# Sample rows of a hybrid decoder step: retention for four heads at once, search products read in PSUM, bias by one-hot products

## The chip, the cores and the metric

The program runs on one core of a Trainium2 chip. The metric is the device time of one execution in microseconds (us). Matmuls and transposes run on TensorE (PE in the profile; PEld is its weight load), elementwise work on VectorE (DVE), ScalarE (ACT) and GpSimd (POOL). SyncE (SP) issues most DMA transfers; POOL issues the gathers, whose row numbers lie in a tile. Every engine works through its own list in order. Matmul results lie in PSUM, of which the kernel uses eight banks; all other tiles lie in SBUF.

## What is computed

One layer of a decoder for two groups of rows that share the weights: a prompt of 1024 positions and 8 sample rows, one for each of 8 sequences with 2048 past positions. First FFN, one projection, sparse attention beside retention, output projection, second FFN, with a layer norm after each. The parts that the change touches belong to the sample rows:

```python
# retention, 4 heads of 128x128 state; for one new position of each sequence:
att = einsum('bihd,bjhd->bhij', qc, kc) * intra
o = einsum('bhij,bjhv->bihv', att, vc) + einsum('bihd,bhdv->bihv', qc, s) * cross_decay
s_new = chunk_decay * s + einsum('bjhd,jh,bjhv->bhdv', kc, kv_decay, vc)
# sparse attention: the 256 best of 2049 keys by the indexer's score, then
logits = einsum('bqhd,bqkhd->bhqk', q, k_sel) * DH_A ** -0.5
bias = rel_bias[t5_bucket(qpos - idx)]          # rel_bias: 32 buckets x 8 heads
p = softmax(where(valid, logits + bias, -inf)); out = einsum('bhqk,bqkhd->bqhd', p, v_sel)
```

A bucket is the number of 31 rising thresholds that the distance reaches.

## The kernel before, in words

All 1032 rows are held transposed, features in the partitions, in three chunks of 344 rows. A product in full precision is made of three fast ones of high and low parts (L169 to L171, L403 to L405). Each weight arrives by SP's transfers (L228), ACT makes its high part (L273) and DVE its low part (L274); up to four raw weights are fetched ahead.

The work is written as generators that a small planner interleaves (`Sched`). The dense products are the main line: each adds its estimated PE time to a clock (`tick`, `g.s.t`), and a generator that gave a delay with `yield` goes on once that time has passed. So the `yield` numbers set where in the program each step of a side job stands. A later pass may move instructions of an engine past each other by its own estimates.

Three side jobs matter. `sret` (L1190) updates the retention state of the sample rows, one sequence after the other, beside the projections of q, k and v: PE spreads a row of v over the partitions (L1069, into a PSUM bank), then for each of four heads ACT multiplies it by that head's key column (L1223, into one small tile `kv`) and DVE adds it to the decayed state (L1224). After a delay the state is stored (L1226), multiplied by the query (L1228), and the state of the sequence after the next is loaded (L1231) into the same half of `sra`.

`s2_select` (L1608) finds the 256 keys of each sequence. Its last part (L1691 on) searches, for each sequence and each half of 128 slots, the position of the selected key: a product into a PSUM bank (L1696), an ACT copy (L1697), four DVE steps (L1698 to L1701). Then the distances become buckets (L1708 to L1710), and 16 gathers on POOL's queue fetch a row of 8 floats of `rel_bias` for each of 128 slots (L1713).

`s3_attend` (L1720) gathers the selected keys and values of the cache (L1730, 32 gathers), forms the logits (L1777, L1778), adds the bias (L1781) and ends with the sample rows of the attention. It begins when `s2_select` has ended and `g.late` is set, which is at the end of the first pass of the output projection. Beside it runs chunk 0 of the second FFN (`plain`, `down`). What waits for its end is the layer norm of chunk 1 (`ln2`) and the job `rest`, which is drained at the end of chunk 0.

Of the kernel before, what the change touches and what calls it, by code (L numbers as in the profile page):

```python
# [17 lines left out]
BF = mybir.dt.bfloat16  # L18
# [4 lines left out]
OP = mybir.AluOpType  # L23
AX = mybir.AxisListType
PSUM = bass.MemoryType.PSUM

P = 128
# [58 lines left out]
def bank(g, kind, name):  # L86

    ks = g.banks[kind]
    t = g.ps.tile([P, 512], F32, tag=f"b{ks[g.bi[kind] % len(ks)]}", name=name, bufs=1)
    g.bi[kind] += 1  # L90
    return t


def bank4(g, kind, name):
    return bank(g, kind, name).rearrange("p (a b) -> p a b", a=4)
# [483 lines left out]
def rsqrt_dve(g, r, v, epsv, u, t):  # L579

    V = g.nc.vector
    ri = r.bitcast(I32)
    V.tensor_scalar(out=u, in0=v, scalar1=epsv, scalar2=None, op0=OP.add)
    V.tensor_scalar(out=ri, in0=u.bitcast(I32), scalar1=1, scalar2=None, op0=OP.arith_shift_right)
    V.tensor_scalar(out=ri, in0=ri, scalar1=-1.0, scalar2=float(0x5F3759DF), op0=OP.mult, op1=OP.add)
    for _ in range(3):
        V.scalar_tensor_tensor(out=t, in0=r, scalar=-0.5, in1=r, op0=OP.mult, op1=OP.mult)
        V.tensor_tensor(out=t, in0=t, in1=u, op=OP.mult)
        V.scalar_tensor_tensor(out=r, in0=t, scalar=1.5, in1=r, op0=OP.add, op1=OP.mult)
# [176 lines left out]
GAM = [float(np.exp(np.log1p(-np.exp2(-5.0 - h)))) for h in range(4)]  # L766
# [89 lines left out]
def cget(g, nm):  # L856
    o, w, r = g.coff[nm]
    return g.csts[0:r, o:o + w]
# [331 lines left out]
def sret(g, smp, state_ret, state_out, mscr, sa, sb):  # L1190

    nc = g.nc
    V = nc.vector
    s2 = [sa[:, q * 512:(q + 1) * 512].rearrange("p (h v) -> p h v", h=4) for q in range(2)]
    cv = Carve(sb, NTOK)
    ks = cv(32).rearrange("p (h b) -> p h b", h=4)
    qm = cv(256).rearrange("p (h b) -> p h b", h=4)
    kv = cv(128)
    vn = Rows(g, [g.ms.tile([40, CW], F32R, tag="silu", name=f"srr{j}", bufs=2)[:, 0:256] for j in range(2)])
    mix = cv(32).rearrange("p (h b) -> p h b", h=4)  # L1200
    st = cv(24, rows=8).rearrange("p (h b) -> p h b", h=4)
    mv = cv(8, rows=8).rearrange("p (h b) -> p h b", h=4)
    rs = cv(4, rows=8)
    V.tensor_scalar(out=ks, in0=smp['k'], scalar1=128.0 ** -0.5, scalar2=None, op0=OP.mult)
    V.memset(qm, 0.0)
    V.tensor_copy(qm[:, :, 0:64:9], smp['q'])
    pt = bank4(g, 'aux', "srvn")
    for h in range(4):
        nc.tensor.transpose(pt[0:8, h, :], smp['v'][:, h, :], g.ident)
    vn.set(pt[0:8].rearrange("p h v -> p (h v)"))  # L1210
    for b in range(2):
        nc.sync.dma_start(s2[b], state_ret[b].rearrange("h d v -> d h v"))
    yield 3.0
    while not g.po_free:
        yield 0.5
    g.po_free -= 1
    po = bank(g, 'po', "sro")
    for b in range(8):
        s0 = s2[b % 2]
        pv = bank(g, 'sc', f"srv{b}")  # L1220
        vn.spread(pv, b)
        for h in range(4):
            nc.scalar.mul(kv, pv[:, h * 128:(h + 1) * 128], ks[:, h, b:b + 1])  # L1223
            V.scalar_tensor_tensor(out=s0[:, h, :], in0=s0[:, h, :], scalar=GAM[h], in1=kv, op0=OP.mult, op1=OP.add)  # L1224
        yield g.sr_step
        nc.sync.dma_start(state_out[b].rearrange("h d v -> d h v"), s0)  # L1226
        for h in range(4):
            nc.tensor.matmul(po[0:8, h * 128:(h + 1) * 128], qm[:, h, b * 8:b * 8 + 8], s0[:, h, :], start=b == 0 and h == 0, stop=b == 7 and h == 3, skip_group_check=True)  # L1228
        g.s.t += 0.9
        if b + 2 < 8:  # L1230
            nc.sync.dma_start(s2[b % 2], state_ret[b + 2].rearrange("h d v -> d h v"))  # L1231
        yield 1.0
    o = s2[0][0:8]
    nc.scalar.copy(o, po[0:8].rearrange("p (h v) -> p h v", h=4))
    g.po_free += 1
    for h in range(4):
        V.bn_stats(out=st[:, h, :], in_=o[:, h, :])
        V.bn_aggr(out=mv[:, h, :], in_=st[:, h, :])
    rsqrt_dve(g, rs, mv[:, :, 1], EPS, st[:, :, 0], st[:, :, 1])
    for h in range(4):  # L1240
        V.tensor_scalar(out=o[:, h, :], in0=o[:, h, :], scalar1=mv[:, h, 0:1], scalar2=rs[:, h:h + 1], op0=OP.subtract, op1=OP.mult)
    yield 4.0
    pt = bank4(g, 'aux', "srpt")
    for h in range(4):
        nc.tensor.transpose(pt[:, h, 0:8], o[:, h, :], g.ident[0:8, 0:8])
    for h in range(4):
        V.scalar_tensor_tensor(out=mix[:, h, :], in0=pt[:, h, 0:8], scalar=g.gng[:, h:h + 1], in1=smp['g'][:, h, :], op0=OP.mult, op1=OP.mult)
    yield 3.0
    nc.sync.dma_start(mscr[:, :, 1024:1032].rearrange("h p b -> p h b"), mix)
# [358 lines left out]
def s2_select(g, sx, ta, tb, out):  # L1608

    nc = g.nc  # L1610
    V = nc.vector
    ca, cb = Carve(ta, NTOK), Carve(tb, NTOK)
    cnt, t, c, T1, lim2, need, lim, limn, nsel, end = (cb(1) for _ in range(10))
    t3, c3, j3 = cb(3), cb(3), cget(g, 'J')[:, 1:4]
    i0, i1, th = (cb(1, I32) for _ in range(3))
    u, sk = ca(130, I32), ca(130, I32)
    hi, lo, jk = ca(130, I16), ca(130, U16), ca(130, BF)
    hi, lo, jk = hi[:, 0:129], lo[:, 0:129], jk[:, 0:129]
# [34 lines left out]
    th = th.bitcast(F32)  # L1653
    ca = Carve(ta, NTOK)
# [16 lines left out]
    n = R[:, 127:128]  # L1671
# [4 lines left out]
    E = cb(256)  # L1676
    V.tensor_scalar(out=E, in0=cget(g, 'J'), scalar1=R[:, 129:130], scalar2=None, op0=OP.is_ge)
    V.scalar_tensor_tensor(out=E, in0=cget(g, 'J'), scalar=end, in1=E, op0=OP.is_lt, op1=OP.mult)
    Rq = [cb(132) for q in range(2)]
# [5 lines left out]
    nc.tensor.matmul(p64[0:64, 0, 1:2], cget(g, 'X0'), nsel, start=True, stop=True)  # L1685
    V.tensor_copy(out['np64'], p64[0:64, 0, 0:2])
    off, pos, row, tj = (cb(16) for _ in range(4))
    gs = cb(132)
    jk = cb(128, BF)
    yield 3.0  # L1690
    for b in range(8):  # L1691
        s = 32 * (b // 2)
        for hf in range(2):
            k = hf * 8 + b
            pg = bank(g, 'aux', f"s2g{b}_{hf}")
            nc.tensor.matmul(pg[:, 0:132], E[s:s + 32, hf * 128:hf * 128 + 128], Rq[b % 2][s:s + 32, :], start=True, stop=True)  # L1696
            nc.scalar.copy(gs, pg[:, 0:132])  # L1697
            V.tensor_tensor(out=tj[:, k:k + 1], in0=cget(g, 'jc')[:, hf:hf + 1], in1=gs[:, 129:130], op=OP.subtract)  # L1698
            V.tensor_scalar(out=jk, in0=gs[:, 0:128], scalar1=tj[:, k:k + 1], scalar2=None, op0=OP.is_le, op1=OP.add, accum_out=off[:, k:k + 1])
            V.tensor_tensor(out=row[:, k:k + 1], in0=off[:, k:k + 1], in1=gs[:, 128:129], op=OP.add)  # L1700
            V.tensor_tensor(out=pos[:, k:k + 1], in0=off[:, k:k + 1], in1=gs[:, 130:131], op=OP.add)  # L1701
            g.s.t += 0.1
            yield 0.8
    V.tensor_copy(out['row'], row)
    V.tensor_scalar(out=pos, in0=pos, scalar1=-1.0, scalar2=2048.0, op0=OP.mult, op1=OP.add)
    ca = Carve(ta, NTOK)
    cv = ca(496).rearrange("p (a b) -> p a b", a=16)
    V.tensor_tensor(out=cv, in0=pos.unsqueeze(2).broadcast_to((P, 16, 31)), in1=cget(g, 'th').unsqueeze(1).broadcast_to((P, 16, 31)), op=OP.is_ge)  # L1708
    V.tensor_reduce(out=off, in_=cv, op=OP.add, axis=AX.X)
    V.tensor_copy(out['bkt'], off)  # L1710
    yield 2.0
    for k in range(16):
        nc.gpsimd.indirect_dma_start(out=out['bias'][:, k, :], out_offset=None, in_=out['rel_bias'], in_offset=bass.IndirectOffsetOnAxis(ap=out['bkt'][:, k:k + 1], axis=0))  # L1713
        yield 1.0


NKEY = 16 * 129
# [166 lines left out]
def trunk(tc, i, o):  # L1884
# [295 lines left out]
    for hd in (1, 2, 3):  # L2180
# [9 lines left out]
        tile(ev_copy(g, t, smp['g'][:, hd, :], AF.Silu), f"gr{hd}")  # L2190
        gT[hd] = t
    sr = s.add(sret(g, smp, i['state_ret'][0], o['ret_state_sample'][0], mscr, A(g, 20, "sra"), A(g, 21, "srb")))


# [49 lines left out]
    def sample():  # L2244

        while not pr[2].done() or s.live(nat):
            yield 0.5
        yield from s2_select(g, sx, A(g, 8, "s2a"), g.z2[:, 0:1024], sel)
        while not g.late:
            yield 0.5  # L2250
        yield from s3_attend(g, sel, smp, i['cache_k'][0].rearrange("n s h d -> (n s) (h d)"), i['cache_v'][0].rearrange("n s h d -> (n s) (h d)"), ascr,
                             dict(ka=o['k_sample'].rearrange("l b s h d -> (l b s) (h d)"), va=o['v_sample'].rearrange("l b s h d -> (l b s) (h d)"), rel_bias=i['rel_bias']),
                             (8, 11, 12), (zt[0][:, 0:1024], zt[0][:, 1024:2048], g.z2[:, 0:1024]))
# [236 lines left out]
```

## Time and profile before

| | |
|---|---|
| median of 3 runs | 2372.45 us (2370.03 to 2373.29) |
| the profiled execution | 2370.71 us, its span 2368.9 us |
| mean granted TensorE clock | 0.977 of full speed |
| busy share: PE, DVE, ACT, POOL | 95%, 75%, 45%, 15% |

The span is what the profile's views divide; the rest of an execution's time lies around it. PE is busy nearly always, so its few gaps and the stretches at a lower granted clock are what to look at. [...]

### The profile page before, as it was taken

To read this page: it belongs to the slowest core of one execution; us is meant where nothing else is said; L and a number is where in the kernel's file an instruction comes from. 1 tells how busy PE (TensorE), PEld (TensorE's weight loads), DVE (VectorE), ACT (ScalarE), POOL (GpSimd) and SP (SyncE) were. 2 spreads that over 40 slices of the span, in tenths; PEclk is the share of its full clock that TensorE was granted. 3 is DMA by queue.
4 is the path that set the end of the run, shared out by engine and by line. 5 is a ranking of instruction groups with operands and counts; after the bars stand their busy time and mean duration, and the time that the engine had idled before them with its cause. 6 is when DMAs were issued, how large, how long until landed. Compare 5 with 4: busy or idle time off the path is not lost.

```text
span 2368.9 us, 37153 instructions
## 1 busy us (share of the span) xinstructions
PE 2239.6 (95%) x14231; PEld 2160.1 (91%) x14231; DVE 1772.9 (75%) x3780; ACT 1076.6 (45%) x1944; POOL 361.2 (15%) x372
## 2 busy tenths in 40 slices
PE   8899999999999998899899999898999899999996
PEld 7899999999998998888689988787999899999995
DVE  4655688787878588777866678876578788887866
ACT  4433343333334466787466665342345443333331
POOL 0000100000002313454023233223220200000003
PEclk9999999999999999999999999998999999999998
DMA  6644322222222201121321242436644321222211
GB/s 176 208 143 142 119 84 81 81 73 71 81 79 101 71 23 51 50 83 47 90 74 49 57 151 72 146 90 153 190 128 145 110 81 63 90 72 74 87 54 48
DMA packets 239370, 224.40 MB, mean 95 GB/s; under 512 B 13291, under 2 KB 219959, under 8 KB 238423
## 3 DMA queue, kind: packets, MB, share of 16 engines
q1 hardware_dynamic: 234838, 209.36, 29.6%
q0 software_dynamic: 4352, 12.65, 2.3%
q8 instruction: 112, 1.84, 0.3%
q14 instruction: 68, 0.55, 0.1%
HBM read 199.40 MB, written 22.58 MB: 94 GB/s over the span
## 4 chain that ended last, share of the span: by engine, by line
PE 73%; DVE 11%; ACT 7%; DMA 3%; issue 3%; POOL 1%; another core or an unknown queue 1%; SPq 0%; POOLq 0%; DVEq 0%; ACTq 0%
PE pds_f L403 4%; PE pds_f L404 4%; PE pds_f L405 4%; ACT ja L1003 3%; PE pdp_f L403 2%; PE pg_f L171 2%; PE pg_f L169 2%; PE pg_f L170 2%; PE pdp_f L404 2%; PE pdp_f L405 2%; PE ps_f2U L169 2%; PE pu_f L169 2%; PE ps_f2U L170 2%; PE ps_f2U L171 2%; PE ps_f1U L169 2%
## 5 line engine op out<-in xcount | busy, mean ns | idle before, releaser
L407 DVE SCALAR_TENSOR_TENSOR z<-pds_f,z 128x344 f32<-128x344 f32 x320 | 164.4, 515 | 137.9 <-PE pds_f L405 137.4
L403 PE MATMUL pds_f<-gs_f,wh_f1ds 128*128 128x344 f32 x352 | 113.8, 324 | 1.7 <-DVE z L407 1.7
L404 PE MATMUL pds_f<-gs_f,wh_f1ds 128*128 128x344 f32 x352 | 113.1, 321 | 0.0
L403 PE MATMUL pds_f<-gs_f,wh_f2ds 128*128 128x344 f32 x352 | 113.0, 321 | 0.0
L404 PE MATMUL pds_f<-gs_f,wh_f2ds 128*128 128x344 f32 x352 | 113.0, 321 | 0.0
L405 PE MATMUL pds_f<-gs_f,wl_f2ds 128*128 128x344 f32 x352 | 112.8, 321 | 0.0
L405 PE MATMUL pds_f<-gs_f,wl_f1ds 128*128 128x344 f32 x352 | 112.7, 320 | 0.0
L407 DVE SCALAR_TENSOR_TENSOR z<-pdp_f,z 128x344 f32<-128x344 f32 x160 | 79.8, 511 | 43.2 <-PE pdp_f L405 42.6
L1003 ACT ACTIVATE ja<-key,zt 128x1024 bf16<-128x1024 int16 (+5 forms) x90 | 93.8, 1042 | 38.2 <-DVE zt L1014 31.0
L684 POOL TENSOR_TENSOR yt<-yt,lot 128x512 f32<-128x512 f32 (+1 forms) x7 | 7.2, 1040 | 548.5 <-DVE lot L677 530.9
L296 ACT CAST wS_f1G<-ws_f1G 128x512 fp32r<-128x512 f32 x44 | 25.1, 619 | 131.4 <-PE pds_f L404 95.2
L296 ACT CAST wS_f2G<-ws_f2G 128x512 fp32r<-128x512 f32 x44 | 25.2, 618 | 129.5 <-PE pds_f L405 120.9
L1468 ACT CAST p<-pT 128x512 fp32r<-128x512 f32 (+2 forms) x112 | 47.4, 433 | 55.8 <-PE pT L1464 43.4
L574 POOL TENSOR_TENSOR lns_l<-z 128x344 f32<-128x344 f32 x3 | 4.1, 1355 | 440.8 <-DVE z L407 430.3
L403 PEld LDWEIGHTS pds_f<-gs_f,wh_f1ds 128*128 128x128 f32 x352 | 66.5, 189 | 3.0 <-DVE z L407 2.2
L404 PEld LDWEIGHTS pds_f<-gs_f,wh_f1ds 128*128 128x128 f32 x352 | 66.5, 189 | 0.3 <-DVE gs_f L466 0.2
L403 PEld LDWEIGHTS pds_f<-gs_f,wh_f2ds 128*128 128x128 f32 x352 | 66.5, 189 | 0.2 <-ACT gs_f L465 0.2
L405 PEld LDWEIGHTS pds_f<-gs_f,wl_f2ds 128*128 128x128 f32 x352 | 66.5, 189 | 0.0
L404 PEld LDWEIGHTS pds_f<-gs_f,wh_f2ds 128*128 128x128 f32 x352 | 66.4, 189 | 0.0
L405 PEld LDWEIGHTS pds_f<-gs_f,wl_f1ds 128*128 128x128 f32 x352 | 66.5, 189 | 0.0
L403 PE MATMUL pdp_f<-gt_f,wh_f2dp 128*128 128x344 f32 x176 | 57.8, 328 | 3.9 <-issue 2.4
L1469 DVE TENSOR_TENSOR p<-pT,p 128x512 fp32r<-128x512 f32 (+2 forms) x112 | 54.4, 496 | 9.2 <-ACT p L1468 8.0
(806 smaller groups left out, 8729.2 us busy)
## 6 DMA issues: line engine op xcount, KB each, us to landing
wr_f1g<-in_ffn_wg_dram SPq DMA_DIRECT2D x22, 512.0 KB
wr_f1u<-in_ffn_wu_dram SPq DMA_DIRECT2D x22, 512.0 KB
wr_f1dp<-in_ffn_wd_dram SPq DMA_DIRECT2D x22, 512.0 KB
wr_f1G<-in_ffn_wg_dram SPq DMA_DIRECT2D x22, 512.0 KB
wr_f1U<-in_ffn_wu_dram SPq DMA_DIRECT2D x22, 512.0 KB
wr_f1ds<-in_ffn_wd_dram SPq DMA_DIRECT2D x22, 512.0 KB
wr_f2u<-in_ffn_wu_dram SPq DMA_DIRECT2D x22, 512.0 KB
wr_f2g<-in_ffn_wg_dram SPq DMA_DIRECT2D x22, 512.0 KB
```

The lines of the kernel that those rows point to most:

```text
L169: g.nc.tensor.matmul(ps, w[0][:, k, :], x[0][:, k, :], start=first and i == 0, stop=False)
L170: g.nc.tensor.matmul(ps, w[0][:, k, :], x[1][:, k, :], start=False, stop=False)
L171: g.nc.tensor.matmul(ps, w[1][:, k, :], x[0][:, k, :], start=False, stop=last and i == n - 1)
L296: nc.scalar.copy(t[:, 0], src)
L403: g.nc.tensor.matmul(ps, wh[:, o, :], th, start=i == 0, stop=False)
L404: g.nc.tensor.matmul(ps, wh[:, o, :], tl, start=False, stop=False)
L405: g.nc.tensor.matmul(ps, wl[:, o, :], th, start=False, stop=i == len(grp) - 1)
L407: g.nc.vector.scalar_tensor_tensor(out=z, in0=ps, scalar=0.5 / ALPHA, in1=z, op0=OP.mult, op1=OP.add)
L684: nc.gpsimd.tensor_tensor(out=yh, in0=yh, in1=mv[0:n, 0:1].broadcast_to((n, 512)), op=OP.subtract)
L1003: nc.scalar.activation(jk[:, 0:n], key[b], AF.Sign, bias=t[:, j:j + 1], scale=-1.0, accum_out=cnt[:, j:j + 1])
L1468: nc.scalar.copy(ph[:, js, ts], ptv[:, js, ts])
L1469: nc.vector.tensor_tensor(out=pl[:, js, ts], in0=ptv[:, js, ts], in1=ph[:, js, ts].bitcast(F32), op=OP.subtract)
```

## The change

In `sret` ACT multiplies the state of each head by its decay in place, and DVE adds the product of v and key for all four heads with two operations over 512 elements; v is read in PSUM and the key columns are broadcast. In the search both halves of a sequence go into one bank, DVE reads it there, and ACT's copy is gone; the delays are the same in sum. For the bias, the comparisons with the thresholds are kept as a 0/1 table (with a column of ones ahead and a column of zeros behind), and the differences of neighbouring columns are a one-hot row of 32 buckets for each of the 16 groups of slots. PE transposes them, four groups at a time, ACT copies the result out, and PE multiplies it by a 128x32 matrix that holds `rel_bias` four times along its diagonal, loaded by four SP transfers. The 16 gathers and their delays of 16 in sum are gone.

```diff
--- before.py
+++ after.py
@@ -1195,7 +1195,7 @@
     cv = Carve(sb, NTOK)
     ks = cv(32).rearrange("p (h b) -> p h b", h=4)
     qm = cv(256).rearrange("p (h b) -> p h b", h=4)
-    kv = cv(128)
+    kv = cv(512).rearrange("p (h v) -> p h v", h=4)
     vn = Rows(g, [g.ms.tile([40, CW], F32R, tag="silu", name=f"srr{j}", bufs=2)[:, 0:256] for j in range(2)])
     mix = cv(32).rearrange("p (h b) -> p h b", h=4)
     st = cv(24, rows=8).rearrange("p (h b) -> p h b", h=4)
@@ -1220,8 +1220,9 @@
         pv = bank(g, 'sc', f"srv{b}")
         vn.spread(pv, b)
         for h in range(4):
-            nc.scalar.mul(kv, pv[:, h * 128:(h + 1) * 128], ks[:, h, b:b + 1])
-            V.scalar_tensor_tensor(out=s0[:, h, :], in0=s0[:, h, :], scalar=GAM[h], in1=kv, op0=OP.mult, op1=OP.add)
+            nc.scalar.mul(s0[:, h, :], s0[:, h, :], GAM[h])
+        V.tensor_tensor(out=kv, in0=pv.rearrange("p (h v) -> p h v", h=4), in1=ks[:, :, b:b + 1].broadcast_to((P, 4, 128)), op=OP.mult)
+        V.tensor_tensor(out=s0, in0=s0, in1=kv, op=OP.add)
         yield g.sr_step
         nc.sync.dma_start(state_out[b].rearrange("h d v -> d h v"), s0)
         for h in range(4):
@@ -1685,33 +1686,50 @@
     nc.tensor.matmul(p64[0:64, 0, 1:2], cget(g, 'X0'), nsel, start=True, stop=True)
     V.tensor_copy(out['np64'], p64[0:64, 0, 0:2])
     off, pos, row, tj = (cb(16) for _ in range(4))
-    gs = cb(132)
     jk = cb(128, BF)
     yield 3.0
+    byb = [v.rearrange("p (f b) -> p b f", f=2) for v in (off, pos, row, tj)]
     for b in range(8):
         s = 32 * (b // 2)
+        pg = bank(g, 'aux', f"s2g{b}")[:, 0:264].rearrange("p (f n) -> p f n", f=2)
         for hf in range(2):
-            k = hf * 8 + b
-            pg = bank(g, 'aux', f"s2g{b}_{hf}")
-            nc.tensor.matmul(pg[:, 0:132], E[s:s + 32, hf * 128:hf * 128 + 128], Rq[b % 2][s:s + 32, :], start=True, stop=True)
-            nc.scalar.copy(gs, pg[:, 0:132])
-            V.tensor_tensor(out=tj[:, k:k + 1], in0=cget(g, 'jc')[:, hf:hf + 1], in1=gs[:, 129:130], op=OP.subtract)
-            V.tensor_scalar(out=jk, in0=gs[:, 0:128], scalar1=tj[:, k:k + 1], scalar2=None, op0=OP.is_le, op1=OP.add, accum_out=off[:, k:k + 1])
-            V.tensor_tensor(out=row[:, k:k + 1], in0=off[:, k:k + 1], in1=gs[:, 128:129], op=OP.add)
-            V.tensor_tensor(out=pos[:, k:k + 1], in0=off[:, k:k + 1], in1=gs[:, 130:131], op=OP.add)
-            g.s.t += 0.1
-            yield 0.8
+            nc.tensor.matmul(pg[:, hf, :], E[s:s + 32, hf * 128:hf * 128 + 128], Rq[b % 2][s:s + 32, :], start=True, stop=True)
+        o, q, r, j = (v[:, b, :] for v in byb)
+        V.tensor_tensor(out=j, in0=cget(g, 'jc'), in1=pg[:, :, 129], op=OP.subtract)
+        for hf in range(2):
+            V.tensor_scalar(out=jk, in0=pg[:, hf, 0:128], scalar1=j[:, hf:hf + 1], scalar2=None, op0=OP.is_le, op1=OP.add, accum_out=o[:, hf:hf + 1])
+        V.tensor_tensor(out=r, in0=o, in1=pg[:, :, 128], op=OP.add)
+        V.tensor_tensor(out=q, in0=o, in1=pg[:, :, 130], op=OP.add)
+        g.s.t += 0.2
+        yield 1.6
     V.tensor_copy(out['row'], row)
     V.tensor_scalar(out=pos, in0=pos, scalar1=-1.0, scalar2=2048.0, op0=OP.mult, op1=OP.add)
+
     ca = Carve(ta, NTOK)
-    cv = ca(496).rearrange("p (a b) -> p a b", a=16)
-    V.tensor_tensor(out=cv, in0=pos.unsqueeze(2).broadcast_to((P, 16, 31)), in1=cget(g, 'th').unsqueeze(1).broadcast_to((P, 16, 31)), op=OP.is_ge)
-    V.tensor_reduce(out=off, in_=cv, op=OP.add, axis=AX.X)
-    V.tensor_copy(out['bkt'], off)
-    yield 2.0
-    for k in range(16):
-        nc.gpsimd.indirect_dma_start(out=out['bias'][:, k, :], out_offset=None, in_=out['rel_bias'], in_offset=bass.IndirectOffsetOnAxis(ap=out['bkt'][:, k:k + 1], axis=0))
-        yield 1.0
+    cv = ca(16 * 34, BF).rearrange("p (a b) -> p a b", a=16)
+    one = ca(512)
+    rbd = ca(32)
+    V.memset(cv[:, :, 0:1], 1.0)
+    V.memset(cv[:, :, 32:33], 0.0)
+    V.memset(rbd, 0.0)
+    for j in range(4):
+        nc.sync.dma_start(rbd[32 * j:32 * j + 32, 8 * j:8 * j + 8], out['rel_bias'])
+    V.tensor_tensor(out=cv[:, :, 1:32], in0=pos.unsqueeze(2).broadcast_to((P, 16, 31)), in1=cget(g, 'th').unsqueeze(1).broadcast_to((P, 16, 31)), op=OP.is_ge)
+    V.tensor_tensor(out=one.rearrange("p (a b) -> p a b", a=16), in0=cv[:, :, 0:32], in1=cv[:, :, 1:33], op=OP.subtract)
+    yield 3.0
+    pt = bank4(g, 'aux', "s2oh")
+    for j in range(4):
+        nc.tensor.transpose(pt[:, j, :], one[:, j * 128:(j + 1) * 128], g.ident)
+    g.s.t += 0.4
+    ot = Carve(tb, 1024)(512).rearrange("p (a b) -> p a b", a=4)
+    nc.scalar.copy(ot, pt)
+    yield 3.0
+    pb = bank4(g, 'aux', "s2bs")
+    for j in range(4):
+        nc.tensor.matmul(pb[:, 0, 32 * j:32 * j + 32], ot[:, j, :], rbd, start=True, stop=True)
+    g.s.t += 0.4
+    V.tensor_copy(out['bias'], pb[:, 0, :].rearrange("p (a b) -> p a b", a=16))
+    yield 1.0
 
 
 NKEY = 16 * 129
```

## Rows read from the trace of the kernel before

**Rows 1.** The page: busy us of the engines (share of the span), instructions.

```profile
PE 2239.6 (95%) x14231; PEld 2160.1 (91%) x14231; DVE 1772.9 (75%) x3780; ACT 1076.6 (45%) x1944; POOL 361.2 (15%) x372
```

**Rows 2.** Stretches: length, busy us (instructions) of PE, PEld, DVE, ACT, POOL; PEclk, DMA, GB/s.

```profile
1590.00:1595.00 5.00, 5.00 (x34) 5.00 (x33) 1.02 (x3) 1.43 (x2) 3.78 (x5) 1.00 0.97 211
1595.00:1600.00 5.00, 3.93 (x22) 2.85 (x21) 1.23 (x2) 1.05 (x1) 4.08 (x4) 1.00 0.91 28
1600.00:1605.00 5.00, 2.48 (x9) 1.36 (x9) 0.00 (x0) 0.00 (x0) 3.78 (x5) 0.52 0.94 108
1605.00:1610.00 5.00, 2.13 (x5) 1.01 (x4) 0.00 (x0) 0.00 (x0) 3.78 (x5) 0.50 0.82 3
1610.00:1615.00 5.00, 1.94 (x5) 1.23 (x5) 1.25 (x1) 0.59 (x2) 1.31 (x2) 0.50 0.92 237
1615.00:1620.00 5.00, 4.29 (x18) 3.43 (x18) 3.31 (x6) 3.30 (x6) 0.00 (x0) 0.78 0.33 99
1620.00:1625.00 5.00, 4.47 (x28) 4.48 (x29) 5.00 (x10) 1.05 (x1) 0.66 (x1) 1.00 0.11 42
```

**Rows 3.** Timeline of POOL: first and last of the 16 bias gathers.

```profile
1587.40 0.94 POOL L1713 DMA_INDIRECT zt<-in_rel_bias_dram,zt  x1 [0.31 <-DVE z L407]
...
1606.92 0.94 POOL L1713 DMA_INDIRECT zt<-in_rel_bias_dram,zt  x1 [0.30 <-issue]
```

**Rows 4.** DMA queues in 1596:1611: packets, MB, share of 16 engines.

```profile
q0 software_dynamic: 378, 0.05, 76.1%
q1 hardware_dynamic: 1043, 0.53, 11.7%
```

**Rows 5.** Timeline of ACT in the same stretch: start, length, instruction, idle before.

```profile
1610.64 0.46 ACT L389 ACTIVATE s_f<-pg_f 128x344 f32<-128x344 f32 x1 [13.75 <-remote]
```

**Rows 6.** Sample retention: waits of 1130:1200, stretches of 10 us, timeline of DVE.

```profile
ACT srb L1223 <- DVE sra L1224: 20.0, 16, 4.0
...
PE sro L1228 <- DVE sra L1224: 6.7, 4, 3.9
...
1140.00:1150.00 10.00, 7.80 (x54) 6.72 (x52) 9.83 (x21) 4.22 (x8) 2.69 (x1) 1.00 0.18 53
1150.00:1160.00 10.00, 8.31 (x37) 5.97 (x38) 8.63 (x27) 3.67 (x8) 0.00 (x0) 0.83 0.29 80
...
1151.37 0.27 DVE L1224 SCALAR_TENSOR_TENSOR sra<-sra,srb 128x128 f32<-128x128 f32 x1
...
1156.87 0.29 DVE L1224 SCALAR_TENSOR_TENSOR sra<-sra,srb 128x128 f32<-128x128 f32 x1 [1.10 <-ACT srb L1223]
```

**Rows 7.** Single lines: duration ns min/median/max, first and last start, shapes.

```profile
L1698 DVE TENSOR_TENSOR zt<-zt x16: 150/154/160, 1532.2 to 1580.2; 128x1 f32<-128x1 f32 x16
L1699 DVE TENSOR_SCALAR_CACHE_REDUCE zt<-zt x16: 337/344/348, 1533.1 to 1581.5; 128x128 bf16<-128x128 f32 x16
L1699 DVE DVE_READ_ACCUMULATOR zt<-zt x16: 81/82/85, 1533.4 to 1581.7; 128x1 f32 x16
...
L1247 DVE SCALAR_TENSOR_TENSOR srb<-srpt,prm,zt x4: 218/218/227, 1205.9 to 1206.4; 128x8 f32<-128x8 f32 x4
...
L589 DVE SCALAR_TENSOR_TENSOR zt<-zt x12: 159/168/173, 860.2 to 1159.0; 128x8 f32<-128x8 f32 x12
```

**Rows 8.** Single lines again: a transpose, and a DVE operation of 512.

```profile
L1181 PE MATMUL pyt<-ident,o x32: 270/272/421, 905.9 to 1162.7; 128*128 128x128 f32 x32
...
L1777 DVE TENSOR_TENSOR s3kv<-s3kv,s3q x16: 664/677/689, 1620.8 to 1661.3; 128x512 f32<-128x512 f32 x16
```

**Rows 9.** Timelines of PE and DVE at the end of the search.

```profile
1576.28 0.49 PE L1696 MATMUL s2g<-zt 32*128 32x132 f32 x2
...
1582.79 0.17 DVE L1705 TENSOR_SCALAR zt<-zt 128x16 f32<-128x16 f32 x1
```

**Rows 10.** Timelines of SP and DVE: a state's load and its first use.

```profile
1177.49 0.54 SPq L1231 DMA_DIRECT2D sra<-in_state_ret_dram  x1
...
1183.15 0.29 DVE L1224 SCALAR_TENSOR_TENSOR sra<-sra,srb 128x128 f32<-128x128 f32 x1 [0.62 <-DMA sra<-in_state_ret_dram]
```

## The prediction

> **What bounds the kernel now.** I read four views, from coarse to fine. First the page: TensorE (PE) is busy 95% of the span [rows 1], so only what PE loses counts, and the question is where it loses. Then a table of equal stretches over the whole span, to find where PE falls short next to the changed lines. [...] Third, the DMA view and the POOL timeline of that hole: POOL issues the 16 bias gathers (L1713) from 1587.40 to 1606.92 [rows 3], and between 1596 and 1611 the queue of POOL's transfers holds 76.1% of the 16 DMA engines' time while it moves 0.05 MB [rows 4]. The other engines stand too: ACT waits 13.75 us, until 1610.64, for something that the profile doesn't name [rows 5], and ACT and DVE have no busy time at all in 1600:1610 [rows 2]. So 2048 pieces of 32 bytes (16 gathers, 128 partitions, one row of 8 floats each) clog what all engines need. Last, the waits and the timeline of the sample retention: ACT and DVE hand one small tile back and forth (ACT waits 20.0 us for DVE), and PE waits 6.7 us for the state, in four waits [rows 6].
>
> **Part 1, the bias gathers go.** At the rate of 1590:1595 the six stretches from 1595 to 1625 would hold 6 x 34 = 204 matmuls; they hold 87 [rows 2]. The 117 missing, at 5 us / 34 = 0.147 us each, are 17 us. At the 31 matmuls in 5 us that I allow for a stage with other work in it, it is 6 x 31 - 87 = 99 missing, at 0.161 us: 16 us. I take **-16**. Before and after the hole PE is full, nothing there follows a clock, and the sample attention that reads the bias is waited for only at the end of chunk 0 of the second FFN, so a later PE program moves up by what the hole cost.
>
> What stays of it: the table is now loaded by four SP transfers of 32 rows, 128 pieces of 32 bytes against 2048. In proportion to pieces that is 16/16 = 1 us, in proportion to transfers 16 x 4/16 = 4 us; none if SP's path doesn't clog. I take **+1** (0 to +4), because the hole's DMA share grows with pieces, not with issues.
>
> [...]
>
> **Part 2, the search products read in PSUM.** ACT loses 16 copies, in a stretch where it is the least busy of the three (1.43 of 5 us in 1590:1595 [rows 2]): 0. DVE: before, 16 times three steps of one element (0.154 each) and a count with its accumulator read (0.344 + 0.082), 14.2 us [rows 7]. After, 8 times one subtraction, two counts with their accumulator reads, two additions: 8 x (3 x 0.154 + 2 x 0.426) = 10.5 us, plus what a PSUM operand adds. That I take from a 128x8 DVE operation that reads PSUM, 0.218, and the nearest one in SBUF, 0.168: 0.05 us for each of 40 operations, 2 us [rows 7]. So 12.5 against 14.2: **0** (-2 to +2), in a stretch where DVE has no slack.
>
> [...]
>
> **Part 3, the bias by one-hot products.** On PE: four transposes and four matmuls, two records each; a 128x128 transpose is 0.272 us [rows 8], so at most 12 x 0.272 = 3.3 us, and about half where they overlap. I take **+2** (+1 to +3). On DVE: a subtraction over 512 (at most 0.677, [rows 8]), three memsets and a PSUM copy come in, a reduction and a conversion go: about +1 us, beside PE. The new wait: PE must wait for the one-hot rows, and DVE runs behind there. The last search product starts on PE at 1576.28, and the DVE step after the loop at 1582.79 [rows 9], 6.5 us later. Behind PE's transposes stand the FFN's matmuls. If the transposes sit where the search ends, PE stands up to 6.5 us; if they sit behind enough FFN matmuls, nothing. The order is written with 3 us of other work ahead of the transposes, and 3 more ahead of the products; I take **+1** (0 to +7). SP's four loads wait for a DVE memset, with the next weight fetches behind them; four weights are fetched ahead, which hides some us: 0. The key gathers on POOL's queue come up by the time of 16 issues, 20 us.
>
> **Part 4, retention for four heads at once.** Per sample DVE had four operations of up to 0.29 [rows 6]; it gets two over 512 elements, each near 0.677 [rows 8]: +0.2 us in length. DVE starts the short ones some 0.2 us apart when nothing holds it and the long ones would be 0.6 apart, so it is up to +0.4, 3 us over eight samples, and DVE is 9.83 of 10 us busy in 1140:1150 [rows 6]. ACT's four multiplications stay, but no longer wait for DVE. What PE waits for: of sample 1 DVE did the four heads at 1151.37, ... and 1156.87 [rows 6], because each needs a trip through ACT; now the sample is whole 1.3 us after DVE gets to it. But the first head's product, which PE waited for longest, now waits for the whole sample, 1 us more. Bounds: the 6.7 us of waits and the 1.7 us of the clock at 0.83 in 1150:1160 [rows 6] all go, -8.4; or each of the eight samples is 0.6 us later, +5. DVE's backlog, not the round trip, sets the longest wait, so I take **-1**.
>
> **The sum.** -16 + 1 + 0 + 2 + 1 - 1 = -13. Against the profiled execution (2370.71, of which the span is 2368.9 and 1.8 lies around it) that is 2357.7; the median of the runs, 2372.45, is 1.7 above it, so the forecast is **2359 us**. A change under 0.2%, 4.7 us, can't be told from none.
>
> **Rivals.**
> 1. The hole is not the bias rows' but that of any burst on POOL's queue, which has 32 more gathers, of keys and values, to issue. For it: PE falls while POOL issues without a pause [rows 3]. Against it: bytes would then be moved, and the queue moves 0.05 MB [rows 4]; and the hole ends some us behind the last bias gather, though the keys follow it. If it stays, the rest is +3 and the time is 2375: no change that can be told.
> 2. Most of the waits go. In part 4 all 8.4 us come back and part 3's wait is hidden: -16 + 1 + 0 + 2 + 0 - 8.4 = -21, **2351**. For it: 20.0 us of ACT waiting for DVE are gone, and ACT also empties PE's banks. Against it: DVE is full.
> 3. The other side: ACT's multiplications now stand at the head of each sample, ahead of the evictions of q, k and v, and wait for the state's load; before, DVE met that wait, once for 0.62 us, 5.66 us after the issue at 1177.49 [rows 10]. If six loads each hold ACT 3 us or more, PE runs out of its two banks and loses 18 us and some 6 at the lower clock: -13 + 24 = +11, **2383**. It decides at a load that lands later than two samples' steps; at 5.66 us against two steps of 7.9 in the trace (four samples from 1151.37 to 1183.15 [rows 6, 10]) it mostly doesn't.
> That the bias is no longer gathered, and that the products go to PSUM once per sample, stands in the code; that the change doesn't do what it says is left out.
>
> **How the numbers follow.** Forecast 0.62, rival 2 0.18, rival 1 0.12, rival 3 0.08. The forecast's own range, with part 3's wait and part 4 at half their bounds, is 2354 to 2365. The range for 8 in 10 takes in rival 2 and part 3's wait at its full bound with the loads of the table, and leaves out rivals 1 and 3: 2347 to 2369. Faster by over 0.2% (under 2367.7): forecast and rival 2, 0.80. Within: rival 1 and the forecast's upper edge, 0.12. Slower: rival 3, 0.08.
>
> **What would show it.** Part 1: near the new L1713's place PE keeps 31 or more matmuls in 5 us, the POOL queue's share falls with its megabytes kept by the keys, and no ACT wait of over 5 us stands there. What remains of the table's load would be a dip of under 1 us. Part 2: no ACT work between the search's products and DVE. Part 3: PE's wait at the transposes is under 3 us, with the clock at 1.00. Part 4: ACT no longer waits for DVE in the retention; PE's waits for the state are under 7 us in total. The prediction is wrong if the hole stays with the gathers gone, if the end doesn't come forward by what the hole cost, or if PE stands at the transposes for 5 us with its clock halved behind it.

## The result, and the profile after

The changed kernel takes **2358.0 us** (median of 6 runs, 2354.8 to 2362.5) against 2372.9 before (6 runs beside it): ratio 0.9938, 95% interval 0.9926 to 0.9951, some 15 us faster. The forecast was 2359 us, with a range of 2347 to 2369. The time was right; the experiments show that its split over the parts was not.

The page of the changed kernel, the line that answers [rows 1]: PE's and ACT's busy time hardly change, POOL loses the bias gathers' 15 us.

```profile
PE 2236.5 (95%) x14243; PEld 2170.3 (92%) x14243; DVE 1774.3 (75%) x3743; ACT 1070.6 (45%) x1929; POOL 346.2 (15%) x356
```

The stretches that answer [rows 2], now behind a search that ends earlier:

```profile
1565.00:1570.00 5.00, 5.00 (x34) 5.00 (x33) 5.00 (x13) 2.22 (x3) 3.33 (x3) 1.00 0.53 157
1570.00:1575.00 5.00, 5.00 (x40) 4.75 (x39) 3.60 (x8) 2.73 (x6) 3.17 (x4) 1.00 1.03 338
1575.00:1580.00 5.00, 5.00 (x35) 4.86 (x34) 4.00 (x7) 3.87 (x6) 0.52 (x1) 1.00 0.71 250
1580.00:1585.00 5.00, 5.00 (x29) 4.20 (x27) 4.80 (x8) 0.55 (x2) 0.24 (x1) 1.00 0.30 105
1585.00:1590.00 5.00, 5.00 (x32) 4.89 (x32) 4.23 (x9) 0.00 (x0) 2.57 (x2) 1.00 0.36 108
```

PE is busy throughout, at clock 1.00, with 29 to 40 matmuls in 5 us: the hole is gone. The POOL queue of the changed kernel in 1566:1581, with the first six key gathers, answers [rows 4]: 1.57 MB in 28.7% of the DMA engines' time, against 0.05 MB in 76.1%.

```profile
q1 hardware_dynamic: 3312, 2.13, 46.5%
q0 software_dynamic: 480, 1.57, 28.7%
```

**Where the time came from.** I set the start of the same PE product in both traces side by side. The change begins at the retention, near 1120; PE's instructions ahead of it are the same, yet the changed kernel's profile stands 6.0 us late there. Over all 12 other kernels below this lead-in is 0.6 to 5.3 us late against the one profile of before, so totals of single profiles don't tell a few us apart; stretches between two marks do:

| from mark to mark (start in before) | changed kernel gains |
|---|---|
| retention, pw_va to srpt (1120.5 to 1204.0) | -5.5 us |
| on to LN2's pm_l (1511.8) | +2.7 |
| on to the next FFN, ps_f2G (1851.9): holds search, bias and attention | -14.1 |
| on to pds_f (1920.6) | -1.4 |

### The profile page after: what moved, and what is told of

Its sections match the earlier page's. It is cut to its first block, busy times and chain, and to the rows that moved or that the text cites. A ratio compares the mean times of both kernels' runs of the same rounds, so it can differ in the third digit from the quotient of the medians.

```text
span 2356.5 us, 37076 instructions
## 1 busy us (share of the span) xinstructions
PE 2236.5 (95%) x14243; PEld 2170.3 (92%) x14243; DVE 1774.3 (75%) x3743; ACT 1070.6 (45%) x1929; POOL 346.2 (15%) x356
## 4 chain that ended last, share of the span: by engine, by line
PE 74%; DVE 11%; ACT 7%; DMA 4%; issue 3%; POOL 1%; SPq 0%; POOLq 0%; DVEq 0%; ACTq 0%
PE pds_f L403 5%; PE pds_f L404 5%; PE pds_f L405 4%; ACT ja L1003 3%; PE pdp_f L403 2%; PE pg_f L169 2%; PE pu_f L169 2%; PE pg_f L171 2%; PE pdp_f L404 2%; PE pg_f L170 2%; PE pdp_f L405 2%; PE pu_f L170 2%; PE pu_f L171 2%; PE ps_f2U L169 2%; PE ps_f2U L170 2%
## 5 line engine op out<-in xcount | busy, mean ns | idle before, releaser
L407 DVE SCALAR_TENSOR_TENSOR z<-pds_f,z 128x344 f32<-128x344 f32 x320 | 164.6, 516 | 141.5 <-PE pds_f L405 141.0
L407 DVE SCALAR_TENSOR_TENSOR z<-pdp_f,z 128x344 f32<-128x344 f32 x160 | 80.2, 512 | 46.7 <-PE pdp_f L405 46.1
L1469 ACT CAST p<-pT 128x512 fp32r<-128x512 f32 (+2 forms) x112 | 47.4, 433 | 55.2 <-PE pT L1465 42.8
L169 PE MATMUL pg_f<-h2h,wh_f2g 128*128 128x344 f32 x176 | 58.5, 332 | 4.6 <-ACT h2h L649 4.6
L169 PE MATMUL pg_f<-xh,wh_f1g 128*128 128x344 f32 x176 | 58.5, 332 | 3.6 <-ACT xh L731 2.8
```

Of the source, the lines that this page charges most:

```text
L169: g.nc.tensor.matmul(ps, w[0][:, k, :], x[0][:, k, :], start=first and i == 0, stop=False)
L407: g.nc.vector.scalar_tensor_tensor(out=z, in0=ps, scalar=0.5 / ALPHA, in1=z, op0=OP.mult, op1=OP.add)
L1469: nc.scalar.copy(ph[:, js, ts], ptv[:, js, ts])
```

## The experiments

The theory that stood after the forecast: the bias gathers' burst makes the hole, so the one-hot part carries the gain. The table has every run; "shift" is the stretch from pm_l to ps_f2G above, against before; the key gathers are those that POOL issues ahead of the 16 bias gathers in the trace.

| kernel | bias gathers | key gathers ahead | us (before, run beside it) | ratio [95%] | shift, us |
|---|---|---|---|---|---|
| before | 16 | 3 | | | 0 |
| changed | 0 | | 2358.0 (2372.9) | 0.9938 [0.9926, 0.9951] | -14.1 |
| only_bias | 0 | | 2368.9 (2371.4) | 0.9990 [0.9981, 0.9998] | -3.6 |
| only_ret | 16 | 3 | 2370.6 (2371.4) | 0.9990 [0.9981, 0.9999] | +4.4 |
| only_search | 16 | 6 | 2360.1 (2371.4) | 0.9943 [0.9930, 0.9957] | -13.8 |
| no_gather | 0 | | 2357.9 (2371.4) | 0.9941 [0.9928, 0.9954] | -15.1 |
| key_first | 16 | 3 | 2360.7 (2370.6) | 0.9951 [0.9938, 0.9965] | -7.2 |
| bias_key_first | 0 | | 2359.0 (2370.6) | 0.9953 [0.9939, 0.9966] | -14.3 |
| gathers_back | 16 | 6 | 2354.3 (2370.6) | 0.9928 [0.9916, 0.9941] | -14.2 |
| no_ret | 0 | | 2358.4 (2370.6) | 0.9950 [0.9938, 0.9963] | -14.0 |
| gs2 | 16 | 4 | 2381.3 (2377.2) | 1.0009 [0.9995, 1.0023] | +5.1 |
| spread32 | 16 | 4 | 2376.1 (2377.2) | 0.9996 [0.9983, 1.0008] | +2.2 |
| after_key_first | 0 | | 2356.5 (2377.2) | 0.9907 [0.9892, 0.9923] | -12.7 |
| back_key_first | 16 | 6 | 2376.9 (2377.2) | 0.9994 [0.9982, 1.0006] | +6.1 |

(The chip of the last four ran the kernel before some 4 to 7 us slower than the others did; compare ratios.)

**One part at a time.** only_bias, only_search and only_ret are the kernel before with one of the change's three hunks each; no_gather leaves the bias out:

```
+    V.memset(out['bias'], 0.0)
     for k in range(16):
-        nc.gpsimd.indirect_dma_start(out=out['bias'][:, k, :], ...
         yield 1.0
```

> The kernel before with the bias part of the change alone: one-hot products in place of the 16 bias gathers; search and retention stay as before. Theory (the hole of the bias gathers carries the gain): -16 + 1 + 2 + 1 = -12 us, about 2361, and PE keeps 30 or more matmuls in each 5 us behind the search. Rival (much of the gain is the retention's, up to -8.4): only -4 to -7 us here, 2366 to 2369.

> The kernel before with the retention part alone (four heads at once); bias gathers and search stay. Theory of the forecast: -1 us, not to be told from none. The profile of the changed kernel, set beside the one before, lets PE's programme come up by about 3.7 us across the retention, which would be -3 to -4. Rival (most of PE's waits for the state go): -8 us, 2365.

> The kernel before with the search part alone (products read in PSUM, two halves at once). Theory: 0 (-2 to +2). Rival: DVE pays a PSUM operand on each of 40 operations in a stretch where it has no slack, and PE's search products wait for it: +3 or more.

> The kernel before with the 16 bias gathers left out and the bias set to zero, so it leaves out the bias of the selected keys; the buckets are still computed. It prices the hole by itself. Theory: -16 to -17 us, 2356, no hole behind the search; less the one-hot kernel's time it gives what the products cost (+2 to +4). Rival (the key gathers, which now start 20 us earlier, bring a hole of their own): 0 to -5.

The hole's price is as forecast, near enough: 13.5 us with the gathers out. But the bias part alone gives 2.5 us and the search part alone, forecast at nothing, 11.3, with all 16 gathers in place. Both theories written for these runs missed that. The DMA burst is there in only_search, and PE doesn't stop:

```profile
1590.00:1595.00 5.00, 5.00 (x34) 5.00 (x33) 3.64 (x5) 2.46 (x3) 3.87 (x4) 1.00 0.39 45
1595.00:1600.00 5.00, 5.00 (x35) 4.86 (x34) 2.07 (x4) 1.45 (x3) 4.00 (x4) 1.00 1.09 219
1600.00:1605.00 5.00, 5.00 (x35) 4.86 (x34) 2.57 (x4) 3.97 (x6) 4.08 (x4) 1.00 0.88 82
```

The timeline of POOL in only_search says what moved. Its first key gather starts at 1574.95, six stand ahead of the first bias gather. Before, three stand ahead and the fourth comes behind the last bias gather [rows 3], at 1608.17. In the source all key gathers stand behind the bias gathers. On POOL they start one after another, 1.25 to 2.18 us apart in this trace; that how many come ahead is settled when the program is built, by the later pass and its estimates, and not by a race in the run, is my reading, which one trace of each program doesn't show.

```profile
1574.95 1.06 POOL L1730 DMA_INDIRECT s3kv<-in_cache_k_dram,zt  x1 [54.66 <-DVE zt L1704]
...
1582.13 0.95 POOL L1730 DMA_INDIRECT s3kv<-in_cache_k_dram,zt  x1 [0.30 <-issue]
1583.38 0.95 POOL L1713 DMA_INDIRECT zt<-in_rel_bias_dram,zt  x1 [0.30 <-DVE s_f L391]
```

The DVE timeline of only_ret names the wait:

```profile
1604.84 0.92 DVE L407 SCALAR_TENSOR_TENSOR z<-pdp_f,z 128x344 f32<-128x344 f32 x2
1618.57 0.69 DVE L1778 TENSOR_TENSOR s3kv<-s3kv,s3q 128x512 f32<-128x512 f32 x1 [12.81 <-DMA s3kv<-in_cache_k_dram,zt]
1619.18 1.22 DVE L274 TENSOR_TENSOR wl_f2g<-wr_f2g,wh_f2g 128x1024 fp32r<-128x1024 f32 x1
```

DVE stands 12.81 us at the first product with key rows; the FFN's work that PE waits for (12.07 us; x0 in 1610:1620) comes behind it, L274 at 1619.18 and L407 at 1620.32. That product's gather goes into a buffer which the search still holds (`kvs` begins with slot 8, which is `s2a`), so it is issued behind the bias gathers, from 1611.04 on in this trace. In only_bias the same wait is 3.8 us, and PE falls to 7 matmuls in 1600:1605 at clock 0.60.

**The new theory, tested.** It says that the hole is that wait, and that the bias gathers cost time only because the key gathers stand behind them. key_first changes nothing but the order of the three buffers, so that the first four key gathers use the two that are free:

```
-                             (8, 11, 12), (zt[0][:, 0:1024], ...
+                             (11, 12, 8), (zt[0][:, 0:1024], ...
```

bias_key_first is only_bias with that line, gathers_back the changed kernel with the hunk of the bias undone, no_ret the changed kernel with the hunk of the retention undone.

> The kernel before with one edit: the three buffers of the key and value gathers are taken in another order, so that the first four key gathers go to the two that are free early and no longer to the one that the search still holds; all 16 bias gathers stay. New theory (the hole is DVE standing in its program at the first key product, whose rows are gathered behind the 16 bias gathers on POOL's queue): the wait of 12.8 to 14.4 us goes, about -11 as in the run with the search part alone, 2360. Rival, the forecast's reason (2048 small pieces clog what all engines need): the hole stays, 0, 2371.

> The kernel before with the bias part and the same other order of buffers. New theory: DVE's wait of 3.8 us for key rows, and PE's stand and low clock behind it (some 7 us), go: -8 to -10 against before, 2362. Rival (what the bias part alone failed to give is the price of its one-hot products): no better than -2.5, 2369.

> The changed kernel with the 16 bias gathers put back in place of the one-hot products; search and retention as changed. New theory (the shorter search brings the first key gathers ahead of the bias gathers, and then these cost little): -10 to -12 against before, 2360, no hole. Rival, the forecast's reason: the gathers carry the gain, so it goes: 0 to -3, 2370.

> The changed kernel with the retention part undone; search and bias as changed. Theory of the forecast, borne out by the retention part alone (0.999): 1 us slower than the changed kernel, 2359. Rival (the two profiles set side by side: PE's programme comes up 3.7 us across the retention): 3 to 4 us slower, 2362.

The first three came out on the new theory's side, bias_key_first and gathers_back with more than it had said; the forecast's reason, that the small pieces clog what all engines need, fell. no_ret, which asks for the retention's share, lies 0.4 us behind the changed kernel by its median and 2.8 by its ratio, between its two theories. key_first gives 9.9 us with all 16 gathers. In it POOL's queue holds most of the DMA engines' time, here in 1600:1615:

```profile
q0 software_dynamic: 333, 0.04, 57.9%
q1 hardware_dynamic: 2240, 2.05, 40.2%
```

PE is full meanwhile, as its stretches show; what is left is one DVE wait of 5.5 us for a later key gather, near 1620:

```profile
1600.00:1605.00 5.00, 5.00 (x37) 4.72 (x36) 2.20 (x3) 3.39 (x5) 3.77 (x5) 1.00 1.05 92
1605.00:1610.00 5.00, 5.00 (x33) 4.42 (x32) 4.10 (x7) 2.58 (x4) 4.09 (x4) 1.00 1.00 212
...
1620.00:1625.00 5.00, 3.00 (x18) 2.47 (x17) 1.78 (x3) 0.00 (x0) 1.03 (x2) 1.00 1.04 349
```

**What makes the search shorter, what makes the packets slow, and does it hold?** gs2 gives ACT's copies two small tiles in turn; spread32 gathers the first 8 numbers of each selected key row, so its bias is not the bias; the other two combine the edits above.

```
-    gs = cb(132)
+    gs2 = [cb(132) for _ in range(2)]
...
+            gs = gs2[hf]
```

```
+    V.tensor_scalar(out=off, in0=row, scalar1=64.0, scalar2=None, op0=OP.mult)
     V.tensor_copy(out['bkt'], off)
...
-        ... in_=out['rel_bias'], ...
+        ... in_=out['kc'], ...
```

> The kernel before with two small tiles in turn in place of one for ACT's copies of the search products; still 16 trips from PE over ACT to DVE. It asks what made the search shorter (52 us from its first product to the row numbers before, 39 with the search part alone). Theory A (the single tile holds PE and ACT for DVE, as ACT's wait of 9.4 us and PE's of 5.5 us there say): the search gets some us shorter, and if six key gathers then stand ahead of the bias gathers, -8 to -11, 2361; if still three, 0 to -3. Theory B (the number of trips sets it): 0, 2371.

> The kernel before with its 16 bias gathers reading other 32-byte pieces: the first 8 numbers of each selected key row, spread over the cache, in place of rows of the one table of 1 KB; so the bias that it adds is not the bias. It asks why a packet of 8 such pieces takes 1.03 us where one of 8 key rows' worth takes 0.159. Theory A (all pieces come from the same few addresses): the packets take 0.3 us or less, the bias gathers land sooner, DVE's wait for the key rows shrinks by some us: -3 to -6. Theory B (the size of the pieces): the packets still take 0.8 to 1.0 us, time 0.

> The changed kernel with the other order of the gathers' buffers. New theory: DVE waits for no key rows there any more, so there is nothing to gain: 0 against the changed kernel, 2358. Rival (the order of buffers helps by itself, whatever stands ahead of it): -3 or more.

> The changed kernel with the 16 bias gathers put back in place of the one-hot products, and the other order of the gathers' buffers. New theory: the wait is gone by either edit, so it equals the run with the gathers put back alone, 2354, and with that one it says whether the one-hot products cost anything against the gathers (some 3 us more for the changed kernel, if the 2354 stands). Rival: the 2354 was chance, and all four versions without the wait lie at 2358.

In gs2 the search takes, from its first product to the row numbers, 1535.2 to 1582.6, 47.4 us, against 52.4 before (1530.3 to 1582.7), 38.8 in only_search (1535.7 to 1574.5) and 32.1 in the changed kernel (1533.5 to 1565.6). So the single tile is some 5 of the 13.6 us, and four key gathers come ahead; the time doesn't fall. The packets of spread32 are fast (median 0.035 us in the packet records, 1.03 before). POOL's queue has 8.0% of the DMA engines' time in 1598:1613, about a tenth of before's share [rows 4]:

```profile
q1 hardware_dynamic: 1253, 0.63, 14.4%
q0 software_dynamic: 383, 0.05, 8.0%
```

Theory A was right on the packets of spread32 (one table isn't all of it: in gs2 the table's own packets take 0.19 us), and wrong on the time, since the hole stays:

```profile
1600.00:1605.00 5.00, 3.09 (x9) 2.38 (x10) 0.97 (x2) 1.04 (x1) 4.08 (x4) 0.77 0.44 108
1605.00:1610.00 5.00, 2.58 (x10) 1.44 (x8) 0.00 (x0) 0.00 (x0) 3.78 (x5) 0.50 0.07 3
1610.00:1615.00 5.00, 2.24 (x6) 1.07 (x4) 0.00 (x0) 0.00 (x0) 3.78 (x5) 0.50 0.16 15
```

Slow packets are thus not what costs the time: hole with a POOL queue at 8.0%, none with it at 57.9%.

back_key_first went against both theories: six key gathers ahead, no wait for key rows, and the whole gain gone. Its DVE timeline:

```profile
1581.14 1.22 DVE L274 TENSOR_TENSOR wl_f2g<-wr_f2g,wh_f2g 128x1024 fp32r<-128x1024 f32 x1
1586.86 0.52 DVE L407 SCALAR_TENSOR_TENSOR z<-pdp_f,z 128x344 f32<-128x344 f32 x1 [4.51 <-remote]
1590.41 0.52 DVE L407 SCALAR_TENSOR_TENSOR z<-pdp_f,z 128x344 f32<-128x344 f32 x1 [3.03 <-PE pdp_f L405]
1600.26 0.52 DVE L407 SCALAR_TENSOR_TENSOR z<-pdp_f,z 128x344 f32<-128x344 f32 x1 [9.34 <-remote]
```

There is a second form of the hole, while the bias gathers are issued (1578.6 to 1597.3). DVE stands 4.51 and 9.34 us without a named cause; PE, which needs the bank that DVE empties, starts again 0.06 us behind DVE's step, after 4.3 and 7.8 us. What DVE waits for is PE's signal: the trace has updates of PE's semaphore at 1586.84, 1590.39, 1600.24 and 1601.69, and in order these belong to products whose last matmuls started at 1581.74, 1582.69, 1589.03 and 1592.58, 5 to 11 us earlier. spread32, gs2 and before show this form too. In before the updates stand at 1610.59 and 1610.62, while the last matmul of the product that ACT waits for ([rows 5], 13.75 us) started at 1595.21; SP, ACT and DVE all start within 0.1 us of them. PE itself drags there: matmuls of one product start 0.7 us apart and more, with no named wait. Timelines of PE, SP and DVE, before:

```profile
1597.78 0.41 PE L169 MATMUL pu_f<-h2h,wh_f2u 128*128 128x344 f32 x1 [0.32 <-issue]
1598.50 0.32 PE L170 MATMUL pu_f<-h2l,wh_f2u 128*128 128x344 f32 x1 [0.30 <-issue]
...
1600.66 0.44 PE L171 MATMUL pu_f<-h2h,wl_f2u 128*128 128x344 f32 x1 [1.00 <-issue]
...
1610.64 0.34 SPq L228 DMA_DIRECT2D wr_f2dp<-in_ffn_wd_dram  x1
...
1610.67 1.25 DVE L274 TENSOR_TENSOR wl_f2g<-wr_f2g,wh_f2g 128x1024 fp32r<-128x1024 f32 x1 [14.43 <-issue]
...
1620.82 0.67 DVE L1777 TENSOR_TENSOR s3kv<-s3kv,s3q 128x512 f32<-128x512 f32 x1
```

The last line is the first product with key rows: in the trace of before DVE doesn't wait for them. The new theory explains only_ret and only_bias; for before itself it is not shown, though the reordered line alone (key_first) takes the hole away.

All kernels with the second form have the 16 gathers; none without them has it; but key_first, only_search and gathers_back have them and not it. Neither the number of key gathers ahead nor the packets' share sorts these from those. What sets it off stays open. One rival is untested, that the recording has a part in it: the trace of before holds 1828 updates of PE's semaphore for the 1832 instructions that raise it, key_first's 1834 for 1832; the other three with this form lack some as well, and so does after_key_first, which has no hole. Nor can the trace of before tell how its loss would divide: only_ret, with the first form in place of the second, takes the same time.

after_key_first takes 2356.5 us, as the changed kernel does within the runs' spread; its ratio lies lower than the changed kernel's, with intervals apart, but on another chip, so the rival isn't excluded.

## Why the prediction was right, and where it was wrong

- **Part 1 (-16, +1 for the table).** The term fits the hole: 14.1 us in the traces, 13.5 with the gathers left out. The +1 came to nothing: the four loads are issued from 1408.1, over 150 us ahead of their use. The reason failed ("2048 pieces clog what all engines need"): the same pieces in the same number leave no hole in only_search and gathers_back. What is shown in its place: one form of the hole is DVE's wait for key rows behind the gathers on POOL's queue, and a second, without a named cause, needs the gathers but doesn't always come with them. 2048 such pieces, 256 packets, took 1.3 us of the 16 engines' time in spread32, spread over the cache, and 13.5 from the 1 KB table in before.
- **Part 2 (0, put down as busy time alone).** The step that failed: alone it gives -11.3 us. The search's latency was left out, 16 trips PE to ACT to DVE through one small tile. Without them the search is 13.6 us shorter, and six key gathers stand ahead of the bias gathers. That these early gathers bring the gain is argued, not shown: gs2 (four ahead) and back_key_first (six) keep a hole of the second form, which is the form in the trace of before. DVE's share was off as well, the other way: an operand in PSUM added next to nothing to these operations, 0.158 against 0.154 us and 0.345 against 0.344 in [rows 7], so the loop is 8 x (0.158 + 2 x 0.428 + 2 x 0.151) = 10.5 us, not 12.5. In the changed kernel (DVE, single lines):

```profile
L1698 DVE TENSOR_TENSOR zt<-zt,s2g x8: 149/158/160, 1534.2 to 1561.9; 128x2 f32<-128x2 f32 x8
L1700 DVE TENSOR_SCALAR_CACHE_REDUCE zt<-s2g,zt x16: 324/345/352, 1534.4 to 1564.7; 128x128 bf16<-128x128 f32 x16
L1700 DVE DVE_READ_ACCUMULATOR zt<-s2g,zt x16: 82/83/85, 1534.7 to 1565.0; 128x1 f32 x16
```

- **Part 3 (+2, +1).** No PE wait for the one-hot rows stands in the trace; ACT waits 0.7 us for the four transposes. In the finished kernel the products cost some 2 us against the gathers by the ratios (0.9938 and 0.9928), which the overlapping intervals don't tell from none. In only_bias the part is far from free, 11.0 us above no_gather; the key rows are late there, and the buffers' order alone takes back 9 to 10 of it.
- **Part 4 (-1).** Right in sign, small in size. In the five profiles with the retention part PE gains 4.1 to 5.5 us across the retention and gives 0.5 to 2.7 back until LN2, 2.2 to 4.6 net (the eight others lie between -0.2 and +1.3 against before); the medians say 0.8 (only_ret) and 0.4 to 2.8 (no_ret, by median and by ratio). The ping-pong of [rows 6] is gone, and PE's four waits for the state, 6.7 us in all, are now one of 3.5 for the bank that DVE reads; a new one of 3.8 stands behind DVE at pw_ka; the third, of 3.6, had one of 4.0 in its place before. The waits of PE in 1126:1215:

```profile
PE pw_ka L169 <- DVE q L1379: 3.8, 1, 3.8
PE srv L1069 <- DVE need L1041: 3.6, 1, 3.6
PE srv L1069 <- DVE srb L1224: 3.5, 1, 3.5
```

- **The rivals.** Rival 1 (any burst on POOL's queue) fell with the key gathers at full PE. Rival 3 fell: ACT waits 1.9 us in all for the state's loads (1.5 the longest). Rival 2's 2351 was not reached.
- **The sum.** Three wrong sizes met: part 2 carries 11 us where none was written, parts 1 and 3 alone 2.5 where 12 were. Parts 1 and 2 each take the same hole away, and their gains don't add: part 2 alone gives 11.3, the bias part with the other order of buffers 11.6, both parts with part 4 give 15. That the total came out within 1 us of the forecast is luck as far as this split goes.

No version beats the changed kernel beyond doubt. gathers_back (2354.3) is as fast or a little faster, but one reordered line brings its hole back (back_key_first), while every kernel with both no bias gathers and early key rows is fast.

## What to carry to other kernels

A hole in which the DMA queue is busy isn't yet the queue's doing (here there was one at 8.0% of the DMA engines' time, in spread32, and none at 57.9%, in key_first): find the instruction at which each engine stands, and ask which transfer it needs and what is ahead of that one on its queue. Cost an edit of a loop by the time until its last result as well as by busy time; what reads that result may be a gather that everything else waits for. And undo the parts one by one even where the sum was right.

## What the runs showed of the hardware

- Pieces of 32 bytes were slower when all came from one table of 1 KB than when spread over the cache: a packet of 256 bytes, 8 pieces, took 1.03 us in before and 0.035 in spread32 (medians of 256 packets). The table's price is not fixed: 0.98 in only_ret, 0.48 in only_search and gathers_back, 0.22 in back_key_first, 0.19 in gs2.
- With the table's packets at 57.9% of the DMA engines, in 1600:1615, PE lost nothing from 1600 to 1620 (key_first): there the high share alone was no loss.
- While 16 indirect transfers were issued, in before mostly 1.25 us apart, PE's semaphore updates came 5 to 11 us (back_key_first) and 15 us (before) behind the start of the matmuls that they belong to in order. Four programs of eight with such a burst had a DVE wait without a named cause in it, the longest 14.43 us in before, 14.4 in spread32, 9.34 in back_key_first and 8.6 in gs2; the cause is open.
- An operand in PSUM cost DVE hardly more than one in SBUF: 0.689 against 0.686 us over 512 elements (the retention's two operations in the changed kernel), 0.345 (changed) against 0.344 (before) over 128.
